# The output projection as seven products, and feed-forward products that add up in single PSUM banks

## The chip, the cores and the metric

The kernel runs on one core of a Trainium2 chip. The metric is the device time of one execution in microseconds, and lower is better. The engines are TensorE (PE, matmuls; PEld is its weight load), VectorE (DVE), ScalarE (ACT), GpSimd (POOL) and the SyncE queue (SP), which issues the loads and stores.

## The reference

One layer of a decoder block on x of 512 tokens and 1024 channels, all in float32. Two token mixers (a spatial gating unit and a gated linear attention) give m; then come the output projection, a layer norm, a feed-forward and a second layer norm:

```python
m = jax.nn.sigmoid(g_a) * y_a + jax.nn.sigmoid(g_b) * y_b
h = layer_norm(DEEPNORM_ALPHA * h + m @ w_out[l], ln1_g[l], ln1_b[l])
f = jnp.square(jax.nn.relu(h @ w_ff1[l])) @ w_ff2[l]
h = layer_norm(DEEPNORM_ALPHA * h + f, ln2_g[l], ln2_b[l])
```

m and w_out are 512 x 1024 and 1024 x 1024; w_ff1 is 1024 x 4096, w_ff2 4096 x 1024. layer_norm subtracts a row's mean, divides by the root of its variance plus 1e-5, multiplies by a gain and adds a bias for each channel.

## The kernel before, in words

Every float32 operand of a matmul is split in two parts that TensorE takes at full speed, high and low: `split` (L88) copies to the high part on ACT and subtracts on DVE for the low part. A product is then three passes: high by high, high by low, low by high (`passes`, L196). Weights come from device memory in chunks of 128 x 1024, in an order written in `_stream` (L1114); `split_to` (L127) splits a chunk into one of 7 buffers, so it runs up to 7 chunks ahead of PE, and `load_to` (L102) keeps the loads ahead of that. 

On PE, DVE, ACT and POOL the instructions stand in the order in which the code emits them (`manual_schedule`); each engine works through its own queue in that order and waits at an instruction whose inputs or buffer are not ready. The loads on SP's queue are placed by the tile framework.

The stages, with PE's work in matmuls of 128 x 128 by 512 columns:

1. Input projections and the two mixers, up to the pairs of gates (`branch`, L821, from 268 us on): for each two channel tiles e, columns of r and of g_B (24 matmuls each), after which ACT applies a SiLU or a sigmoid and DVE multiplies and adds into m (`r_take`, `gb_take`). Each tile of m is then split (L827, L855).
2. The output projection: two halves of 512 channels (`row_unit`, L199, with `out_take`, L863). For each half and each of the 4 token tiles it runs 8 x 3 matmuls into a bank of PSUM; DVE then adds alpha times x (L869) and takes row statistics (L870). After the second half `ln_apply` (L635) does the layer norm of a row: aggregate, a power on POOL (L171), and two steps of 1024 columns on DVE with gain and bias. `turn_h` (L878) transposes a token tile of h on PE (8 matmuls with the identity) into PSUM, and ACT and DVE split it into hh and hl.
3. The feed-forward's hidden layer, 512 hidden columns at a time (`block`, L922; the first in two parts of 256 tokens, L1006), and for three quarters of it (pairs 0 to 2) the second product in seven products in place of eight (`seven_products`, L967). F and w_ff2 are cut in 2 x 2 blocks; sums of blocks of w_ff2 are made on DVE by `sum_to` (L119), sums of blocks of F by `operand` (L935). A product has two token tiles of 12 matmuls. `keep` (L955) adds each product to its own accumulator in SBUF, and `together` (L993) combines the accumulators near the end. A product alternates with a hidden column job of 24 matmuls.
4. The last quarter in plain order (L1066 on) with the second layer norm. The last token tile's 1024 channels are done in pieces of 512, 384 and 128.

PSUM has 8 banks: `ps_m` 4, `ps_s` 2 and `ps_a` 2 (L84 to L86).

Of the kernel before, what the change touches and what calls it, by code (L numbers as in the profile page):

```python
# [15 lines left out]
P = 128  # L16
T = 512
# [29 lines left out]
def hybrid_block(  # L47
# [13 lines left out]
    ln1_b: bass.AP,  # L61
    ln2_g: bass.AP,
# [22 lines left out]
    ps_s = pool(ctx, "ps_s", bufs=1, space=PSUM)  # L85
    ps_a = pool(ctx, "ps_a", bufs=2, space=PSUM)  # L86
# [11 lines left out]
    raws, chunks, kept = {}, {}, {}  # L98
    lanes, ring = {0: rpool}, {lane: [] for lane in LANES}
    state = {"load": 0, "sum": 0, "split": 0}  # L100

    def load_to(n):  # L102
        while state["load"] < min(n, NCHUNK):
            i = state["load"]
            kind, lane, key, news = STREAM[i]
            if news is not None:
                ends = ring[lane]
                if len(ends) >= LANES[lane] and ends[-LANES[lane]] >= state["split"]:
                    break
                raw = lanes[lane].tile([P, 1024], F32, name=f"raw{i}", tag="raw")  # L110
                nc.sync.dma_start(raw, w_all[news])
                kept.setdefault(key, []).append(raw)
                users = [j for j in range(i + 1, NCHUNK) if STREAM[j][2] == key]
                users = [j for n_, j in enumerate(users) if all(STREAM[x][3] is None for x in users[:n_])]
                ends.append(max([i] + (users if key else [])))
            raws[i] = kept[key][-1:] if kind == "one" else kept[key][-2:]
            state["load"] = i + 1

    def sum_to(n):  # L119
        while state["sum"] < min(n, state["load"]):  # L120
            i = state["sum"]
            raw, *other = raws[i]
            if other:
                nc.vector.tensor_tensor(raw, raw, other[0], op=ALU.add if STREAM[i][0] == "sum" else ALU.subtract)  # L124
            state["sum"] = i + 1

    def split_to(n):  # L127
        n += n > ASIDE
        while state["split"] < min(n, NCHUNK):
# [8 lines left out]
            raw = raws[i][0]  # L138
# [4 lines left out]
        load_to(n + sum(LANES.values()) if 1 in lanes else n + RAW_BUFS)  # L143
# [106 lines left out]
    for i in range(4):  # L250
        raws[i] = [None]
# [542 lines left out]

    def r_take(e, t1):
# [41 lines left out]
    lnp.tile([P, 32], F32, name="pad_n")  # L837
    first_ln = ExitStack()
    ln1p = pool(first_ln, "ln1p", side="right")
    g1 = row_bcast(ln1p, ln1_g, D, "g1")  # L840
    b1 = row_bcast(ln1p, ln1_b, D, "b1")
    mstack = ExitStack()
    mpool = pool(mstack, "mpool", side="left")
    mh = mpool.tile([P, KT, T], F32R, name="mh")
    ml = mpool.tile([P, KT, T], F32R, name="ml")

    def turn(src, t, half, dh, dl):

        pt = ps_a.tile([P, 4, P], F32, name="pturn", tag="aux")
        for i in range(4):  # L850
            nc.tensor.transpose(pt[:, i, :], src[:, (half * 4 + i) * P : (half * 4 + i + 1) * P], ident)
        ks, tsl = slice(half * 4, half * 4 + 4), slice(t * P, (t + 1) * P)
        split(dh[:, ks, tsl], dl[:, ks, tsl], pt)

    for e in range(2):  # L855
        split(mh[:, e, :], ml[:, e, :], AT_[:, e, :])
    for e in range(2, KT, 2):
        branch(e)


    hh, hl = xh, xl

    def out_take(half):  # L863
        def f(t, ps):
            sl = slice(half * 512, (half + 1) * 512)
            xr = mpool.tile([P, 512], F32, name=f"xr{half}_{t}", tag="xr", bufs=3)
            nc.sync.dma_start(xr, x[t * P : (t + 1) * P, sl])
            z = bufA[:, t, sl]
            nc.vector.scalar_tensor_tensor(z, xr, ALPHA, ps, op0=ALU.mult, op1=ALU.add)  # L869
            nc.vector.bn_stats(st1[t][:, half, :], z)  # L870
            if half:
                ln_apply(
                    bufA[:, t, :], bufA[:, t, :], st1[t].rearrange("p a b -> p (a b)"), g1, b1, ln1p, f"l1{t}"
                )

        return f

    def turn_h(t):  # L878
        for half in range(2):
            turn(bufA[:, t, :], t, half, hh, hl)  # L880

    row_unit(mh, ml, out_take(0))
    at(S_O + 5, lambda: turn_h(0))
    at(S_O + 6, lambda: turn_h(1))
    row_unit(mh, ml, out_take(1))
    mstack.close()
    first_ln.close()
# [18 lines left out]
    lanes[1] = pool(seven, "rpool2", side="right", bufs=LANES[1])  # L910
    op = pool(seven, "op", side="left", bufs=2)
    sub = lambda o, x_, y_: nc.vector.tensor_tensor(o, x_, y_, op=ALU.subtract)  # L912
# [22 lines left out]
    def operand(F, p, m):  # L935
        a = lambda i, j: F[:, j - 1, :, (i - 1) * 256 : i * 256]
        x_, *y_ = {
            5: (a(1, 2), a(1, 1)),
            1: (a(1, 1), a(2, 2)),
            3: (a(1, 1),),  # L940
            4: (a(2, 2),),
            6: (a(2, 1), a(1, 1)),
            7: (a(1, 2), a(2, 2)),
            2: (a(2, 1), a(2, 2)),
        }[m]
        if y_:
            d_ = op.tile([P, 4, 256], F32, name=f"d{p}_{m}", tag="d", bufs=1)
            sub(d_, x_, y_[0])
            x_ = d_
        hi = op.tile([P, 4, 256], F32R, name=f"oh{p}_{m}", tag="oh")  # L950
        lo = op.tile([P, 4, 256], F32R, name=f"ol{p}_{m}", tag="ol")
        split(hi, lo, x_)
        return hi, lo

    def keep(p, m, t, ps):  # L955
        dst = acc[m][:, t, :]
        if p == 0 and m in (6, 7):
            h = quarter(bufA, *((1, 1) if m == 6 else (0, 0)))[:, t, :]
            nc.vector.scalar_tensor_tensor(dst, h, ALPHA, ps, op0=ALU.mult, op1=ALU.add)
        elif p == 0:  # L960
            nc.scalar.copy(dst, ps)
        else:
            nc.vector.tensor_add(dst, dst, ps)

    made = {}

    def seven_products(F, p, F_next):  # L967
# [4 lines left out]
        def job(n):  # L972
            m = ORDER[n]
# [4 lines left out]
            hi, lo = made.pop((p, n))  # L978
            u0 = take_chunks(2)
            for t in range(2):  # L980
                tsl = slice(t * P, (t + 1) * P)
                ps = ps_m.tile([P, 512], F32, name=f"m{p}_{m}_{t}", tag="ps")
                for k in range(4):
                    wh, wl = (c.rearrange("p (k n) -> p k n", k=2)[:, k % 2, :] for c in chunks[u0 + k // 2])
                    for i, (s_, m_) in enumerate(passes(hi[:, k, tsl], lo[:, k, tsl], wh, wl)):
                        nc.tensor.matmul(ps, s_, m_, start=(k == 0 and i == 0), stop=(k == 3 and i == 2))  # L986
                    if t and k % 2:
                        split_to(u0 + k // 2 + 1 + W_BUFS)
                keep(p, m, t, ps)

        return [lambda n=n: job(n) for n in range(7)]

    def together(m, t, terms, h=None):  # L993

        z = acc[m][:, t, :]
        for sign, n in terms:
            nc.vector.tensor_tensor(z, z, acc[n][:, t, :], op=ALU.add if sign > 0 else ALU.subtract)
        if h:
            nc.vector.scalar_tensor_tensor(
                z, quarter(bufA, *h)[:, t, :], ALPHA, z, op0=ALU.mult, op1=ALU.add  # L1000
            )
# [11 lines left out]
    for job in block(take_raw(F, 1)):  # L1013
        job()
# [210 lines left out]
```

## Time and profile before

| | us |
|---|---|
| median of 3 runs | 758.21 |
| lowest and highest | 758.09, 758.42 |
| the profiled execution | 757.96 |
| its span, first to last instruction | 756.2 |
| PE busy in the span | 747.2 |
| output projection on PE | 367.3 to 412.6 |
| feed-forward, hidden tokens of the second half from | 426.3 |

A row of the timeline has the start in us, the duration, the engine, the line, the operation and its tiles. The duration of a matmul is its latency; matmuls follow each other faster than that, so their cost is the step from one start to the next. A row of the list of groups has the count, the busy time, the mean of one in ns, and the idle time before it. A row of the table by windows has the stretch, then busy time (and instructions) of PE, PEld, DVE, ACT and POOL, the granted TensorE clock, the DMA share and GB/s. A row of the list of waits has who waited, for whom, us in total, times, the longest.

### The profile page before, as it was taken

Reading aid. Unit: us, or ns where it says so; the run is one execution under the profiler, and the core shown is the slowest. Engines: PE = TensorE matmul, PEld = TensorE weight load, DVE = VectorE, ACT = ScalarE, POOL = GpSimd, SP = SyncE. Lnnn points to the kernel's source line nnn. Section 1 sums busy time; section 2 is a strip of 40 time slices with the busy share of each in tenths; the row PEclk is TensorE's granted clock in tenths of the full one; section 3 lists DMA queues with packets and bytes.
Section 4 is the critical chain, followed back from the end, with each engine's and each line's share of the span. In section 5 each row is a group of like instructions: output and inputs, shape, how many; then the busy total and the mean of one; then the engine's idle time right before and its main releaser. Section 6 shows DMA issues by size and latency. Waiting matters only on the chain.

```text
span 756.2 us, 8829 instructions
## 1 busy us (share of the span) xinstructions
PE 747.2 (99%) x3498; PEld 626.8 (83%) x3498; DVE 492.8 (65%) x618; ACT 349.5 (46%) x472; POOL 29.8 (4%) x60
## 2 busy tenths in 40 slices
PE   9999999999999999999999999999999999999996
PEld 7878888888888888888888988888888888888885
DVE  8478876676575554435458544874677667777995
ACT  7475744363254735444222544454644444445300
POOL 1000000000000102000002000000000000000011
PEclk9999999999999999999999999999999999999998
DMA  8623422222142131432341423444234333534111
GB/s 341 208 73 125 137 77 80 84 84 84 36 141 75 56 126 56 144 107 84 98 158 33 171 62 107 139 140 140 86 137 141 137 112 112 164 114 166 58 56 55
DMA packets 25465, 85.15 MB, mean 113 GB/s; under 512 B 3088, under 2 KB 3344, under 8 KB 25424
## 3 DMA queue, kind: packets, MB, share of 16 engines
q1 hardware_dynamic: 25280, 84.33, 32.4%
q8 instruction: 27, 0.44, 0.2%
q10 hardware_dynamic: 144, 0.26, 0.1%
q14 instruction: 14, 0.11, 0.1%
HBM read 82.48 MB, written 2.10 MB: 112 GB/s over the span
## 4 chain that ended last, share of the span: by engine, by line
PE 96%; issue 1%; DVE 1%; DMA 0%; POOL 0%; DVEq 0%; POOLq 0%
PE f L691 22%; PE ps L213 17%; PE m L986 15%; PE f L1077 6%; PE gb L691 6%; PE r L691 6%; PE ga L691 6%; PE u L691 6%; PE qk L691 3%; PE first L272 3%; PE sc L519 2%; PE pm L744 1%; PE po L553 1%; PE po L557 1%; PE po L555 1%
## 5 line engine op out<-in xcount | busy, mean ns | idle before, releaser
L90 DVE TENSOR_TENSOR wl<-raw,wh 128x1024 fp32r<-128x1024 f32 x141 | 171.2, 1222 | 99.2 <-ACT wh L89 97.7
L89 ACT CAST wh<-raw 128x1024 fp32r<-128x1024 f32 x141 | 145.7, 1044 | 51.1 <-PE ps L213 23.7
L691 PE MATMUL f<-xh,wh 128*128 128x512 f32 (+1 forms) x288 | 105.4, 366 | 0.0
L691 PE MATMUL f<-xl,wh 128*128 128x512 f32 (+1 forms) x288 | 105.3, 365 | 0.0
L691 PE MATMUL f<-xh,wl 128*128 128x512 f32 (+1 forms) x288 | 105.2, 365 | 0.0
L986 PE MATMUL m<-wh,oh 128*128 128x512 f32 x168 | 65.4, 389 | 0.0
L986 PE MATMUL m<-wl,oh 128*128 128x512 f32 x168 | 65.4, 389 | 0.0
L986 PE MATMUL m<-wh,ol 128*128 128x512 f32 x168 | 65.4, 389 | 0.0
L691 PEld LDWEIGHTS f<-xh,wl 128*128 128x128 f32 x288 | 54.3, 189 | 8.8
L691 PEld LDWEIGHTS f<-xh,wh 128*128 128x128 f32 x288 | 54.3, 189 | 8.7
L691 PEld LDWEIGHTS f<-xl,wh 128*128 128x128 f32 x288 | 54.3, 189 | 8.6
L213 PE MATMUL ps<-wh,xh 128*128 128x512 f32 x128 | 50.4, 394 | 0.0
L213 PE MATMUL ps<-wh,xl 128*128 128x512 f32 x128 | 49.8, 389 | 0.0
L213 PE MATMUL ps<-wl,xh 128*128 128x512 f32 x128 | 49.8, 389 | 0.0
L915 ACT ACTIVATE F<-f 128x512 f32<-128x512 f32 (+1 forms) x28 | 15.0, 536 | 70.7 <-PE f L691 70.7
L124 DVE TENSOR_TENSOR raw<-raw,raw 128x1024 f32<-128x1024 f32 x30 | 36.6, 1221 | 9.1 <-DMA raw<-in_w_all 9.1
L986 PEld LDWEIGHTS m<-wh,ol 128*128 128x128 f32 x168 | 31.5, 188 | 6.6
L986 PEld LDWEIGHTS m<-wh,oh 128*128 128x128 f32 x168 | 31.5, 188 | 6.6
L986 PEld LDWEIGHTS m<-wl,oh 128*128 128x128 f32 x168 | 31.5, 188 | 6.5
L89 ACT CAST oh<-d 128x1024 fp32r<-128x1024 f32 x15 | 15.7, 1049 | 36.4 <-DVE d L912 36.4
L90 DVE TENSOR_TENSOR ol<-d,oh 128x1024 fp32r<-128x1024 f32 x15 | 18.4, 1225 | 16.7 <-ACT oh L89 16.7
L213 PEld LDWEIGHTS ps<-wh,xl 128*128 128x128 f32 x128 | 24.0, 188 | 5.1
(231 smaller groups left out, 1477.1 us busy)
## 6 DMA issues: line engine op xcount, KB each, us to landing
raw<-in_w_all SPq DMA_DIRECT2D x136, 512.0 KB, 3.3
bufB<-in_head SPq DMA_DIRECT2D x4, 512.0 KB, 7.9
xr<-in_x SPq DMA_DIRECT2D x8, 256.0 KB, 3.6
out<-bufA SPq DMA_DIRECT2D x8, 256.0 KB, 2.0
bufA<-in_head SPq DMA_DIRECT2D x3, 512.0 KB, 5.3
brow<-in_b_in SPq DMA_DIRECT2D x4, 256.0 KB, 6.4
g<-in_ln_g SPq DMA_DIRECT2D x2, 512.0 KB, 4.0
b<-in_ln_b SPq DMA_DIRECT2D x2, 512.0 KB, 4.9
```

The lines of the kernel that those rows point to most:

```text
L89: nc.scalar.copy(hi, src)
L90: nc.vector.tensor_tensor(lo, src, hi.bitcast(F32), op=ALU.subtract)
L124: nc.vector.tensor_tensor(raw, raw, other[0], op=ALU.add if STREAM[i][0] == "sum" else ALU.subtract)
L213: nc.tensor.matmul(ps, s_, m_, start=(k == 0 and i == 0), stop=(k == KT - 1 and i == 2))
L272: nc.tensor.matmul(first[e], s_, m_[:, k, :], start=(k == 0 and i == 0), stop=(k == KT - 1 and i == 2))
L519: nc.tensor.matmul(sc[:, c, 0:192], pr.kt[:, jc * P : (jc + 1) * P], pr.qt[:, jc, :], start=True, stop=True)
L553: nc.tensor.matmul(po, pr.AT[:, j, c, :], vs, start=True, stop=(c == 0))
L555: nc.tensor.matmul(po, pr.QI[:, j, c * P : (c + 1) * P], pr.S[j], start=False, stop=True)
L691: nc.tensor.matmul(ps, s_, m_, start=(k == 0 and i == 0), stop=(k == KT - 1 and i == 2))
L915: nc.scalar.activation(dst, ps, AF.Relu)
L986: nc.tensor.matmul(ps, s_, m_, start=(k == 0 and i == 0), stop=(k == 3 and i == 2))
L1077: nc.tensor.matmul(ps, s_, m_, start=(f == 0 and i == 0), stop=(f == 7 and i == 2))
```

## The change

**The projection in seven products.** m is 4 k-tiles by 2 block columns, 256 tokens by 2 block rows; w_out is stored in quarters like w_ff2. `product_of` runs one product of 2 x 12 matmuls, for the projection and the feed-forward alike. The order of products and what they add to are new:

```python
ORDER = (1, 2, 5, 6, 3, 7, 4)
PAIRED = ((0, 1), (4, 5), (2, 6), (3, 7))
...
GOES = {1: (0, 0), 2: (0, 0), 5: (1, 1), 6: (0, 1), 3: (0, 1), 7: (1, 1), 4: (1, 0)}
NEW = (1, 5, 6, 4)
```

GOES gives the quarter of the result (token half, channel half). Products 1, 6, 7 and 4 add up in the same two banks x (one for each token tile), 5 and 3 in two banks v, and 2 has banks of its own; DVE adds the state of the bank to the quarter after each product, so a bank may not be added to further before DVE has read it. `ps_s` and `ps_a` end after the gates, and the four banks x and v take their place; v also takes the transposed tiles.

```diff
+    def accumulators(m, name):
+        if m in (1, 6, 7, 4):
+            if m == 1:
+                sums["x"] = [ps_t.tile([P, 512], F32, name=f"mx{name}_{t}", tag=f"x{t}") for t in range(2)]
+            return sums["x"], m == 1
+        if m in (5, 3):
+            if m == 5:
+                sums["v"] = [ps_t.tile([P, 512], F32, name=f"mv{name}_{t}", tag=f"v{t}") for t in range(2)]
+            return sums["v"], m == 5
+        return [ps_m.tile([P, 512], F32, name=f"m{name}_{t}", tag="ps") for t in range(2)], True
```

**Operands.** The gates are done in the order PAIRED, so that both channel tiles of a k-tile are there; after each pair the operands of that k-tile are made: three blocks are split as they are, and four sums of 256 columns are made and split (`summed`). The blocks of w_out and w_ff2 are subtracted in place in four held buffers (`A0`, `A1`, `B0`, `B1`), and the chunk stream has 14 chunks for the projection where there were 8.

```diff
+    def summed(k):
+        a = lambda i, j: AT_[:, k + 4 * (j - 1), (i - 1) * 256 : i * 256]
+        d = [temp(f"ms{k}_{i}").rearrange("p (m t) -> p m t", m=2) for i in range(2)]
+        (s1, s2), (s4, s3) = [(x_[:, 0, :], x_[:, 1, :]) for x_ in d]
+        nc.vector.tensor_tensor(s1, a(2, 1), a(2, 2), op=ALU.add)
+        for o, x_, y_ in ((s2, s1, a(1, 1)), (s4, a(1, 2), s2), (s3, a(1, 1), a(2, 1))):
+            nc.vector.tensor_tensor(o, x_, y_, op=ALU.subtract)
+        for i in range(2):
+            split(mh[:, 2 * i : 2 * i + 2, k, :], ml[:, 2 * i : 2 * i + 2, k, :], d[i])
```

**The first layer norm.** Token tiles 0 and 1 are normalised on ACT without gain and bias; these are applied on channels after the transpose, by eight ACT instructions of 128 x 128 in PSUM for a tile, and much later in rows on DVE for the residual. Tiles 2 and 3 keep the form in rows.

```diff
+    def turn_h(t):
+        for half in range(2):
+            pt = ps_t.tile([P, 4, P], F32, name="pturn", tag=f"v{half}")
+            for i in range(4):
+                e = half * 4 + i
+                nc.tensor.transpose(pt[:, i, :], bufA[:, t, e * P : (e + 1) * P], ident)
+            for i in range(4 if t < 2 else 0):
+                e = half * 4 + i
+                g_, b_ = ln1c[:, e : e + 1], ln1c[:, 8 + e : 9 + e]
+                nc.scalar.activation(pt[:, i, :], pt[:, i, :], AF.Identity, bias=b_, scale=g_)
+            ks, tsl = slice(half * 4, half * 4 + 4), slice(t * P, (t + 1) * P)
+            split(hh[:, ks, tsl], hl[:, ks, tsl], pt)
+
+    def project_take(m, t, ps):
+        i, j = GOES[m]
+        dst, tt = quarter(bufA, i, j)[:, t, :], 2 * i + t
+        if m in NEW:
+            xr = mpool.tile([P, 512], F32, name=f"xr{m}_{t}", tag="xr", bufs=3)
+            nc.sync.dma_start(xr, x[tt * P : (tt + 1) * P, j * 512 : j * 512 + 512])
+            nc.vector.scalar_tensor_tensor(dst, xr, ALPHA, ps, op0=ALU.mult, op1=ALU.add)
+        else:
+            nc.vector.tensor_add(dst, dst, ps)
+        if m in (2, 3, 7, 4):
+            stats(tt, j)
+        if m == 3:
+            rest_of_stats(tt)
+            if t:
+                normalise(0)
+        if m == 7:
+            if t:
+                normalise(1)
+            else:
+                turn_h(0)
+        if m == 4:
+            st = st1[tt].rearrange("p a b -> p (a b)")
+            ln_apply(bufA[:, tt, :], bufA[:, tt, :], st, *rows1["gb"], lnp, f"l1{tt}")
+            if t == 0:
+                turn_h(1)
```

**The feed-forward.** Its 3 x 7 products keep their number and size, with the new order, operands and banks; `keep` adds every product to its quarter at once, and `together` and its accumulators go. The gain and bias of tiles 0 and 1 are multiplied and added in rows on DVE during the second hidden block.

```diff
-        pieces = ((0, 512), (512, 512)) if t < NT - 1 else ((0, 512), (512, 384), (896, 128))
+        pieces = ((0, 512), (512, 512)) if t < NT - 1 else ((0, 512), (512, 256), (768, 256))
```

Besides, the weights of the low-rank gate (`als`) take one of the 7 weight buffers early on and are split in whole, and the scratch area for DMA is smaller.

**Where instructions moved.** On DVE, from the last gate's addition into m (first row). Before, wl is the low part of a chunk, ml that of m; L869 and L870 are the addition and the statistics of a token tile:

```order
L817 TENSOR_TENSOR bufA<-bufA,gb_2829 128x512
L90 TENSOR_TENSOR wl_2834<-raw_2727,wh_2833 128x1024
L90 TENSOR_TENSOR ml<-bufA,mh 128x512
L869 SCALAR_TENSOR_TENSOR bufA<-xr_0_2866,ps_0_2841 128x512
L870 BN_STATS st_0_2360<-bufA 128x6
L869 SCALAR_TENSOR_TENSOR bufA<-xr_1_2895,ps_1_2870 128x512
L870 BN_STATS st_1_2361<-bufA 128x6
```

And after the change, from the same addition to the first of product 1 (L959); L130 subtracts chunks of weights, L910 and L912 make the sums of m:

```order
L867 TENSOR_TENSOR bufA<-bufA,gb_2848 128x512
L130 TENSOR_TENSOR raw_2441<-raw_2691,raw_2441 128x1024
L91 TENSOR_TENSOR wl_2853<-raw_2439,wh_2852 128x1024
L91 TENSOR_TENSOR ml<-bufA,mh 128x256
L910 TENSOR_TENSOR ms_0_2861<-bufA 128x256
L912 TENSOR_TENSOR ms_0_2861<-ms_0_2861,bufA 128x256
L912 TENSOR_TENSOR ms_1_2862<-bufA,ms_0_2861 128x256
L912 TENSOR_TENSOR ms_1_2862<-bufA 128x256
L91 TENSOR_TENSOR ml<-ms_0_2861,mh 128x2x256
L91 TENSOR_TENSOR ml<-ms_1_2862,mh 128x2x256
L91 TENSOR_TENSOR ml<-bufA,mh 128x256
L959 SCALAR_TENSOR_TENSOR bufA<-xr_0_2892,mxo_0_2878 128x512
```

Ten instructions stand between the last gate and the projection's first addition where there were two.

On DVE at the end of the projection, before: the third token tile's second half with its layer norm, the low parts of a turned tile (xl), then chunks of weights:

```order
L869 SCALAR_TENSOR_TENSOR bufA<-xr_2_3092,ps_2_3067 128x512
L870 BN_STATS st_2_2362<-bufA 128x6
L638 BN_AGGR mv_l_3096<-st_2_2362 128x2
L168 TENSOR_SCALAR rs_l_3097<-mv_l_3096 128x1
L640 SCALAR_TENSOR_TENSOR bufA<-bufA,mv_l_3096,g_2372 128x1024
L646 SCALAR_TENSOR_TENSOR bufA<-bufA,rs_l_3097,b_2374 128x1024
L90 TENSOR_TENSOR xl<-pturn,xh 128x4x128 x2
L90 TENSOR_TENSOR wl_3125<-raw_2951,wh_3124 128x1024
```

After, from product 7's second tile (mxo is a bank x) over product 4's first tile with its layer norm to the low parts of token tile 1:

```order
L961 TENSOR_TENSOR bufA<-bufA,mxo_1_2879 128x512
L930 BN_STATS st_3_2343<-bufA 128x6
L959 SCALAR_TENSOR_TENSOR bufA<-xr_0_3182,mxo_0_2878 128x512
L930 BN_STATS st_2_2342<-bufA 128x6
L640 BN_AGGR mv_l_3186<-st_2_2342 128x2
L175 TENSOR_SCALAR rs_l_3187<-mv_l_3186 128x1
L642 SCALAR_TENSOR_TENSOR bufA<-bufA,mv_l_3186,mf_2962 128x1024
L648 SCALAR_TENSOR_TENSOR bufA<-bufA,rs_l_3187,mf_2964 128x1024
L91 TENSOR_TENSOR xl<-pturn,xh 128x4x128 x2
```

Here xl is token tile 1, and the hidden layer's first part needs it; half a product of PE's work (12 matmuls) stands between its turn and that part where a whole group (24 matmuls) stood.

On PE, the first turn before and after (pturn is the transposed tile):

```order
L213 MATMUL ps_1_3017<-wh_2935,mh 128x512
L213 MATMUL ps_1_3017<-wl_2936,mh 128x512
L213 MATMUL ps_1_3017<-wh_2935,ml 128x512
L851 MATMUL pturn<-ident,bufA 128x128 x8
L213 MATMUL ps_2_3067<-wh_2761,mh 128x512
```

```order
L832 MATMUL mxo_0_2878<-wh_2989,mh 128x512
L832 MATMUL mxo_0_2878<-wl_2990,mh 128x512
L832 MATMUL mxo_0_2878<-wh_2989,ml 128x512
L945 MATMUL pturn<-ident,bufA 128x128 x8
L832 MATMUL mxo_1_2879<-wh_2953,mh 128x512
```

The turn of token tile 0 now stands behind product 7's first tile, that of tile 1 behind product 4's first tile.

More of the change, by code (lines that the diff above doesn't have):

```diff
@@ L96, in hybrid_block @@
     ASIDE = NCHUNK - 3
-    raws, chunks, kept = {}, {}, {}
-    lanes, ring = {0: rpool}, {lane: [] for lane in LANES}
+    chunks, kept, ring = {}, {}, []
+    held, held_to = {}, {}
     state = {"load": 0, "sum": 0, "split": 0}
@@ L104, in load_to @@
             i = state["load"]
[L105 to L108, printed above, removed]
+            c, own, *_ = STREAM[i]
+            if c is not None and own is None:
+                if len(ring) >= RAW_BUFS and ring[-RAW_BUFS] >= state["split"]:
                     break
[L110 to L116, printed above, removed]
+                kept[i] = rpool.tile([P, 1024], F32, name=f"raw{i}", tag="raw")
+                ring.append(i)
+            elif c is not None:
+                if "pool" not in held or held_to.get(own, -1) >= state["split"]:
+                    break
+                kept[i] = held[own] = held["pool"].tile([P, 1024], F32, name=f"raw{i}", tag=own)
+                held_to[own] = max(j for j in range(i, min(i + 40, NCHUNK)) if STREAM[j][3] == STREAM[i][3] and own in STREAM[j][2:])
+            if c is not None:
+                nc.sync.dma_start(kept[i], w_all[c])
             state["load"] = i + 1
@@ L121, in sum_to @@
             i = state["sum"]
-            raw, *other = raws[i]
-            if other:
-                nc.vector.tensor_tensor(raw, raw, other[0], op=ALU.add if STREAM[i][0] == "sum" else ALU.subtract)
+            _, own, dst, _, less = STREAM[i]
+            if dst is not None:
+                raw = held[dst]
+                if less:
+                    x_, y_ = (held[a] if a else kept[i] for a in less)
+                    nc.vector.tensor_tensor(raw, x_, y_, op=ALU.subtract)
+                kept[i] = raw
             state["sum"] = i + 1
@@ L142, in split_to @@
             state["split"] = i + 1
[L143 removed]
+        load_to(n + RAW_BUFS + 2)
     xh = xpool.tile([P, KT, T], F32R, name="xh")
@@ L843, in hybrid_block @@
     mpool = pool(mstack, "mpool", side="left")
[L844 to L858, printed above, removed]
-    hh, hl = xh, xl
[L863 to L876, printed above, removed]
+    mh = mpool.tile([P, 6, 4, 256], F32R, name="mh")
@@ L977, in job @@
                 made[p + 1, 0] = operand(F_next, p + 1, ORDER[0])
[L978 to L989, printed above, removed]
-        return [lambda n=n: job(n) for n in range(7)]
[L993 to L1001, printed above, removed]
+            product_of(f"{p}_{ORDER[n]}", ORDER[n], made.pop((p, n)), keep(p))
+        return [lambda n=n: job(n) for n in range(7)]
     F = fp.tile([P, 2, 4, T], F32, name="F0", tag="F")
@@ L1118, in _stream @@
     n = 15 * 4
-    out = [("one", 0, None, None)] * 4 + [("one", 0, None, c) for c in range(n)]
+    out = [(None, None, None, None, None)] * 4 + [(c, None, None, None, None) for c in range(n - 8)]
     f1 = n
@@ L1142, in _stream @@
             out += take(1 + (i == 0)) + product
-    out += [("one", 0, None, f2 + 8 * PAIRS + c) for c in range(8 * (DF // 1024 - PAIRS))]
+    out += [(f2 + 8 * PAIRS + c, None, None, None, None) for c in range(8 * (DF // 1024 - PAIRS))]
     return out
```

219 lines of the change are left out of this document (118 added, 101 removed).

## The prediction

> **What bounds the kernel now.** I read the page first: PE's row, then the list of what PE waits for.
>
> ```profile
> PE 747.2 (99%) x3498; PEld 626.8 (83%) x3498; DVE 492.8 (65%) x618; ACT 349.5 (46%) x472; POOL 29.8 (4%) x60
> ```
>
> ```profile
> PE wu L248 <- POOL bal L294: 1.1, 1, 1.1
> PE pt L408 <- PE ps L213: 0.6, 1, 0.6
> ```
>
> Nothing here is long: PE is busy 99% of the span and never waits in the stages that the change touches. So the time is PE's own work, as long as the other engines stay ahead. The chain prices that work.
>
> ```profile
> 367.46 32.64 PE ps L213 x144
> ...
> 470.64 5.44 PE m L986 x24
> ```
>
> 144 matmuls in 32.64 us and 24 in 5.44 us are both 0.2267 us for a matmul of 512 columns. The table by windows shows how far DVE is from PE: in the last gates, in the output projection, in the feed-forward.
>
> ```profile
> 290.00:367.40 77.40, 77.40 (x355) 64.16 (x354) 34.85 (x42) 35.94 (x51) 3.55 (x8) 1.00 0.29 100
> 367.40:411.00 43.60, 43.60 (x202) 36.28 (x201) 27.08 (x36) 10.54 (x13) 4.56 (x3) 1.00 0.29 96
> ```
>
> ```profile
> 465.00:704.50 239.50, 239.50 (x1058) 198.30 (x1057) 172.55 (x166) 122.34 (x153) 0.00 (x0) 1.00 0.39 132
> ```
>
> DVE (third number) has 27.08 us of work in the projection's 43.60 and 172.55 of 239.50 in the feed-forward.
>
> **What PE saves.** The projection goes from 8 x 24 = 192 matmuls to 7 x 24 = 168. That is 24 x 0.2267 = 5.44 us less. The feed-forward keeps its 21 products. At the end the last row's pieces change.
>
> ```profile
> 742.52 0.33 PE L1077 MATMUL f<-wh,Fs 128*128 128x384 f32 x1
> ...
> 746.71 0.22 PE L1077 MATMUL f<-wh,Fs 128*128 128x128 f32 x1
> ...
> 749.22 0.28 PE L1077 MATMUL f<-wh,xl 128*128 128x128 f32 x1
> ```
>
> ```profile
> 423.33 0.36 PE L691 MATMUL f<-xh,wh 128*128 128x256 f32 x1
> 423.53 0.28 PE L691 MATMUL f<-xl,wh 128*128 128x256 f32 x1
> 423.65 0.29 PE L691 MATMUL f<-xh,wl 128*128 128x256 f32 x1
> ```
>
> The pieces of 384 and 128 columns take 742.52 to 749.33, 6.8 us. Two of 256 take 48 x 0.12 = 5.8 us (0.12 is the step from 423.53 to 423.65). The last piece's add and statistics on DVE double in width, about 0.14 us each by the next two rows. Net -0.8 us.
>
> ```profile
> L1078 DVE TENSOR_TENSOR bufB<-bufB,f 128x128 f32<-128x128 f32 x1 | 0.3, 289 | 1.5 <-PE f L1077 1.5
> ```
>
> ```profile
> L480 DVE TENSOR_TENSOR dr<-dr,k 128x256 f32<-128x256 f32 x4 | 1.7, 425 | 0.1
> ```
>
> **What DVE pays.** Before, the projection's 192 matmuls used 8 chunks of weights; now 168 use 14, of which 8 are first made by a subtraction. DVE works strictly in the order of its queue. Its prices by the step from one start to the next:
>
> ```profile
> 478.96 1.22 DVE L124 TENSOR_TENSOR raw<-raw,raw 128x1024 f32<-128x1024 f32 x1
> 480.10 1.22 DVE L90 TENSOR_TENSOR wl<-raw,wh 128x1024 fp32r<-128x1024 f32 x1
> ...
> 486.07 0.68 DVE L959 SCALAR_TENSOR_TENSOR bufB<-bufA,m 128x512 f32<-128x512 f32 x1
> 486.72 1.22 DVE L90 TENSOR_TENSOR wl<-raw,wh 128x1024 fp32r<-128x1024 f32 x1
> ```
>
> 1.14 us for 1024 columns, 0.65 for 512, some 0.37 for 256. Let 0 be the first matmul of product 1:
>
> ```profile
> 367.30 0.39 PE L213 MATMUL ps<-wh,mh 128*128 128x512 f32 x1
> ```
>
> Nothing on PE ahead of it changes, and DVE is up to date there: the operands cost it 4 x (7 x 0.37 + 2 x 0.65) = 16 us in place of 8 x 0.65 = 5, and the window from 290 has 42 us free. But the last gate ends at 0 too, and its work cannot start earlier: PE's result at 0.2, the sigmoid 0.7 (row below), DVE at 0.9. From there to the addition of product 3's first tile its queue holds 34 instructions: 14 of 1024 columns (10 splits, 4 sums: 16.0 us), 12 of 512 (7.9), 2 statistics (1.4), 6 of 256 (2.2). That is 27.5 us and 0.3 of dependent gaps: DVE is there at 28.8. PE has finished that tile at 24.6. **DVE is 4.2 us late**, and the rest follows from that. The single bank for products 5 and 3 bites first: product 3's second tile may not be added to it before DVE has read product 5's, at 25.2; PE is there at 24.5 and waits 0.8.
>
> Then row 0's layer norm, priced from today's:
>
> ```profile
> 394.70 0.69 DVE L869 SCALAR_TENSOR_TENSOR bufA<-xr,ps 128x512 f32<-128x512 f32 x1 [1.36 <-PE ps L213]
> 395.42 0.69 DVE L870 BATCH_NORM_STATS2 st<-bufA 128x6 f32<-128x512 f32 x1
> 396.15 0.21 DVE L638 BATCH_NORM_AGGREGATE mv_l<-st 128x2 f32<-128x12 f32 x1
> 396.39 0.15 DVE L168 TENSOR_SCALAR rs_l<-mv_l 128x1 f32<-128x1 f32 x1
> 396.46 1.28 DVE L640 SCALAR_TENSOR_TENSOR bufA<-bufA,mv_l,g 128x1024 f32<-128x1024 f32 x1
> ```
>
> ```profile
> 396.63 1.52 POOL L171 TENSOR_TENSOR rs_l<-rs_l,nhalf 128x1 f32<-128x1 f32 x1 [95.34 <-DVE rs_l L168]
> ```
>
> ```profile
> L171 POOL TENSOR_TENSOR rs_sg<-rs_sg,nhalf 128x1 f32<-128x1 f32 x4 | 2.2, 551 | 63.9 <-DVE rs_sg L168 63.9
> ...
> L654 POOL TENSOR_SCALAR rs_sg<-mv_sg,rs_sg 128x1 f32<-128x1 f32 x4 | 1.1, 264 | 0.4
> ```
>
> ```profile
> L673 ACT ACTIVATE bufB<-bufB,rs_sg 128x1024 f32<-128x1024 f32 x4 | 4.9, 1233 | 0.0
> ...
> L815 ACT ACTIVATE gb<-gb,cols_sb 128x512 f32<-128x512 f32 x8 | 5.5, 689 | 22.1 <-PE gb L691 22.1
> ```
>
> 28.8 + 1.84 on DVE (394.70 to 396.54) + 1.52 on POOL = 32.2. The same power takes 0.551 where DVE is idle, and 1.52 where a long DVE instruction runs: it ended 0.41 after that instruction. Now two splits run there back to back, so I let POOL's second instruction (0.264 alone) end after the second, at 33.2; alone it would be 32.5. Then 1.23 on ACT, and PE may turn row 0 at **34.6** (or 33.8). Without waits PE would be there after 11 half products, at 29.9.
>
> [...]
>
> From that turn to the first hidden tile, DVE and ACT alternate:
>
> ```profile
> 415.48 1.04 PE L851 MATMUL pturn<-ident,bufA 128*128 128x128 f32 x8
> ```
>
> ```profile
> L580 ACT ACTIVATE bufB<-po,ss 128x256 f32<-128x256 f32 x16 | 6.8, 470 | 0.2 <-POOL ss L171 0.2
> ```
>
> ```profile
> L915 ACT ACTIVATE F<-f 128x256 f32<-128x256 f32 x8 | 3.1, 383 | 9.6 <-PE f L691 9.6
> ```
>
> ```profile
> L89 ACT CAST xh<-pturn 128x512 fp32r<-128x512 f32 x8 | 4.4, 584 | 13.8 <-PE pturn L851 13.8
> ```
>
> The scale and shift on channels is 8 new ACT instructions for each of two rows, 128x128 in PSUM; no row shows one. Half of a 256-column step is 0.10 (584 less 383, halved), so 0.28 without and 0.37 with a pointer (470). I take 0.37, and 0.03 between, as each waits for the last. A row then costs ACT 2 x (4 x 0.40 + 0.55) = 4.3. Row 0: 34.6 + 0.7 + 4.3 = 39.6; two casts and splits of weights behind it, DVE free at 43.0. Only then come, in DVE's order: the addition and statistics of product 7's second tile, the same of product 4's first (2.8), aggregate and scalar (0.4), the 1024-column step (1.28), the wait for POOL (0.4), the next (1.28), and at last row 1's low part, 0.65: **49.7**. Meanwhile PE does two half products, a turn, a half product (10.2 us, and a wait of 1.7 for row 1's normalisation on ACT) and stands at 46.5, as the hidden tile's second matmul needs that low part: 3.2 us of wait. Four hidden parts and two turns later (4 x 2.88 + 2 x 1.04 = 13.6) the second half of the hidden tokens starts at 63.3. Before it is 423.33 + 24 x 0.12 = 426.3, or 59.0. **The stage is 4.3 us longer:** 5.4 saved, 9.7 of waits. With POOL's lower price and 0.28 the same count gives 61.9 (+2.9); with DVE 3% slower, 64.5 (+5.5).
>
> **What costs nothing.** From there the feed-forward hides the rest: sums fall from 10 to 8 a pair, operands from 5 subtractions to 4, the last additions (20 x 0.68) go, ten copies of ACT's become DVE's additions (6.5 us) and four 1024-column steps come for the late scale and shift (4.6 us); DVE had 67 us free. Its banks are used once more after a full hidden job, 8.2 us of slack. If that cover went, DVE's lag beyond 8.2 us would fall on PE. The loads behind the held buffers on SP's queue wait for DVE's splits at 18.0 and 22.4, and what stands behind them is wanted at 25.4 or later. The early low-rank weights only change their place.
>
> **The sum.** Against the profiled execution, 757.96 (span 756.2): +4.3 - 0.8 = +3.5, between +2.1 and +4.7. The median is 758.21, 0.25 above; on it the forecast is 761.7.
>
> **Rivals.** First, the gain arrives: PE gets 5.4 and 0.8 us, **752.0**. It decides at the low part of row 1: DVE would have to be through it by about 40, not 49.7. For it: PE waits nowhere today, DVE has 16.5 us free in this stage, and the loads are early. Against it: the count above, in which no step is dearer than today's, and the strict order of the queue. 0.16.
>
> Second, DVE goes through its queue about 8% faster than its steps today; the same count then starts the second half near 59: **757 to 759.5**, no change. Against it: the steps are the same to 1% wherever I looked. 0.15.
>
> Third, PE's waits halve its clock. After the last matmul the granted clock fell:
>
> ```profile
> 751.00:752.00 1.00, 0.00 (x0) 0.00 (x0) 1.00 (x3) 0.00 (x0) 0.68 (x1) 0.91 0.00 0
> 752.00:753.00 1.00, 0.00 (x0) 0.00 (x0) 1.00 (x2) 0.00 (x0) 0.00 (x0) 0.50 0.00 0
> ```
>
> 0.91 over one microsecond is a fall at 751.8, 2.3 us after PE's end at 749.5. Waits of 3.9 and 3.2 us are longer. At half speed the first would be swallowed by PE's later waits; behind the second a hidden part takes 2.88 us more: **764.6**. 0.15. [...]
>
> **How the numbers follow.** Forecast 0.54, rivals 0.16, 0.15, 0.15. A measurement tells about 0.2%, 1.5 us, from no change. Faster 0.16, within 0.15, slower 0.54 + 0.15 = 0.69. The range leaves out the first rival and little else: 757.0 to 765.0; the forecast's own is 760.3 to 762.9.
>
> **What would show it.** Right: PE waits in product 3, 3 to 4 us before the first turn, 1 to 2 before the second, about 3 at the first hidden part, and no waits later; POOL's power near 1.5; the scale and shift near 0.37. Wrong: the first turn follows its half product without a gap, or DVE reaches product 3's addition before 25, or PE waits in the feed-forward.

## The result and the profile after

| | before | after |
|---|---|---|
| median, us | 758.13 (6 runs) | 762.05 (6 runs) |
| lowest and highest | 757.87, 758.42 | 761.51, 763.62 |
| the profiled execution, its span | 757.96, 756.2 | 761.6, 759.5 |

The ratio is 1.0055, with a 95% interval of 1.0045 to 1.0065: 0.55% slower. The runs of the changed kernel lie 2.1 us apart, those of the kernel before 0.55.

The page, first the busy times. PE is busy 4.2 us less than the 747.2 of before (24 matmuls fewer, but some at a clock of 0.50, see below), in a span that is 3.3 us longer.

```profile
PE 743.0 (98%) x3474; PEld 622.3 (82%) x3474; DVE 502.7 (66%) x640; ACT 362.5 (48%) x485; POOL 29.7 (4%) x62
```

The list of what PE waits for has three rows that were not there before (in all, times, the longest), all in the stretch that the change made new.

```profile
PE pturn L945 <- ACT bufA L937: 5.2, 2, 3.2
PE f L693 <- DVE xl L91: 1.3, 1, 1.3
...
PE mvo L832 <- DVE bufA L959: 0.2, 1, 0.2
```

The table by windows for the gates, the projection with the first hidden tiles, and the feed-forward (PE, PEld, DVE, ACT, POOL, then the granted clock). Only the middle stretch has a PE below its length, and only there is the clock below 1.00.

```profile
290.00:366.00 76.00, 76.00 (x349) 63.02 (x348) 43.15 (x64) 38.91 (x60) 3.55 (x8) 1.00 0.26 87
366.00:429.00 63.00, 56.25 (x293) 47.37 (x292) 55.20 (x75) 33.29 (x53) 6.08 (x6) 0.97 0.53 190
465.00:707.00 242.00, 242.00 (x1069) 200.44 (x1068) 169.64 (x167) 117.59 (x143) 0.00 (x0) 1.00 0.36 122
```

The chain that ended last has the same piece in both kernels, behind the last turn: the rest of the hidden tiles, 264 matmuls. Its start is called the link below. Before:

```profile
423.57 47.06 PE f L691 x264
```

After, with the start of the low part of row 1 that the first hidden tile waits for:

```profile
415.99 0.69 DVE xl L91
416.73 3.01 PE f L693 x23
...
427.65 47.06 PE f L693 x264
```

Product 1 starts at 367.30 before and at 367.49 after (each kernel's zero in what follows):

```profile
367.49 0.39 PE L832 MATMUL mxo<-wh,mf 128*128 128x512 f32 x1
```

So the link comes 56.3 after zero before and 60.2 after: the stage is 3.9 us longer. From the link to the end of the span it is 756.2 - 423.57 = 332.6 before and 759.5 - 427.65 = 331.9 after, 0.8 less. With the 0.2 us of a later zero that is the 3.3 us of the spans.

Where the stage's time goes, on the timelines of DVE, POOL, ACT and PE:

```profile
391.62 0.68 DVE L959 SCALAR_TENSOR_TENSOR bufA<-xr,mvo 128x512 f32<-128x512 f32 x1
392.21 0.68 DVE L959 SCALAR_TENSOR_TENSOR bufA<-xr,mxo 128x512 f32<-128x512 f32 x1
...
395.08 0.68 DVE L959 SCALAR_TENSOR_TENSOR bufA<-xr,mxo 128x512 f32<-128x512 f32 x1
395.68 0.68 DVE L961 TENSOR_TENSOR bufA<-bufA,mvo 128x512 f32<-128x512 f32 x1
396.39 0.69 DVE L930 BATCH_NORM_STATS2 st<-bufA 128x6 f32<-128x512 f32 x1
...
397.45 2.36 DVE L91 TENSOR_TENSOR wl<-raw,wh 128x1024 fp32r<-128x1024 f32 x2
...
401.48 0.68 DVE L961 TENSOR_TENSOR bufA<-bufA,mxo 128x512 f32<-128x512 f32 x1
402.19 0.69 DVE L930 BATCH_NORM_STATS2 st<-bufA 128x6 f32<-128x512 f32 x1
```

```profile
397.60 1.48 POOL L178 TENSOR_TENSOR rs_l<-rs_l,nhalf 128x1 f32<-128x1 f32 x1 [96.13 <-DVE rs_l L175]
399.18 0.76 POOL L656 TENSOR_SCALAR rs_l<-mv_l,rs_l 128x1 f32<-128x1 f32 x1
401.65 0.55 POOL L178 TENSOR_TENSOR rs_l<-rs_l,nhalf 128x1 f32<-128x1 f32 x1 [1.71 <-DVE rs_l L175]
402.30 0.27 POOL L656 TENSOR_SCALAR rs_l<-mv_l,rs_l 128x1 f32<-128x1 f32 x1
```

```profile
399.97 1.24 ACT L937 ACTIVATE bufA<-bufA,rs_l 128x1024 f32<-128x1024 f32 x1 [2.86 <-POOL rs_l L656]
401.96 1.82 ACT L949 ACTIVATE pturn<-pturn,ln1c 128x128 f32<-128x128 f32 x4 [0.75 <-PE pturn L945]
...
406.64 1.99 ACT L90 CAST wh<-raw 128x1024 fp32r<-128x1024 f32 x2
```

```profile
401.27 1.09 PE L945 MATMUL pturn<-ident,bufA 128*128 128x128 f32 x8 [3.16 <-ACT bufA L937]
...
409.83 1.71 PE L945 MATMUL pturn<-ident,bufA 128*128 128x128 f32 x8 [1.99 <-ACT bufA L937]
...
416.73 0.39 PE L693 MATMUL f<-xl,wh 128*128 128x256 f32 x1 [1.33 <-DVE xl L91]
```

DVE reaches product 3's first addition 28.2 after zero. From there statistics, POOL's two instructions and ACT's normalisation stand in a line up to the first turn at 33.8, while two splits of weights go on beside them on DVE. POOL's power and its small instruction take 1.48 and 0.76 us for row 0, beside these splits, and 0.55 and 0.27 for row 1, beside the addition at 401.48 and the statistics at 402.19.

By microseconds, the clock falls to half right behind the second wait:

```profile
410.00:411.00 1.00, 1.00 (x7) 1.00 (x7) 0.97 (x3) 0.27 (x1) 0.00 (x0) 0.57 0.86 279
411.00:412.00 1.00, 1.00 (x5) 0.91 (x4) 0.99 (x2) 0.93 (x3) 0.00 (x0) 0.50 0.83 266
412.00:413.00 1.00, 1.00 (x3) 0.76 (x3) 0.90 (x2) 0.94 (x3) 0.00 (x0) 0.50 0.69 209
413.00:414.00 1.00, 1.00 (x5) 0.77 (x4) 1.00 (x2) 0.93 (x4) 0.76 (x1) 0.72 0.71 279
```

0.43 + 0.50 + 0.50 + 0.28 = 1.7 us of PE's work lost. The sum of the stage: at the first turn, the second turn, the first hidden part and product 3 the steps from start to start are 3.3, 2.2, 1.5 and 0.4 us longer than without the waits (each step is some 0.16 us longer than its wait: a matmul's duration of 0.39 less its step of 0.23), in all 7.4; with the half clock 9.1; less the 5.4 us saved 3.7, of 3.9 measured.

### The profile page after: what moved, and what is told of

It reads as the page before. It is cut to its first block, busy times and chain, and to the rows that moved or that the text cites. A ratio compares the mean times of both kernels' runs of the same rounds, so it can differ in the third digit from the quotient of the medians.

```text
span 759.5 us, 8842 instructions
## 1 busy us (share of the span) xinstructions
PE 743.0 (98%) x3474; PEld 622.3 (82%) x3474; DVE 502.7 (66%) x640; ACT 362.5 (48%) x485; POOL 29.7 (4%) x62
## 4 chain that ended last, share of the span: by engine, by line
PE 92%; DVE 4%; issue 1%; ACT 1%; DMA 1%; POOL 0%; DVEq 0%; ACTq 0%
PE f L693 23%; PE ps L220 11%; PE mx L832 9%; PE f L1127 6%; PE gb L693 6%; PE r L693 6%; PE ga L693 6%; PE u L693 6%; PE mv L832 4%; PE qk L693 3%; PE first L277 3%; PE m L832 2%; PE sc L521 2%; DVE wl L91 1%; PE pm L746 1%
## 5 line engine op out<-in xcount | busy, mean ns | idle before, releaser
L91 DVE TENSOR_TENSOR wl<-raw,wh 128x1024 fp32r<-128x1024 f32 x147 | 178.1, 1222 | 107.3 <-ACT wh L90 105.8
L90 ACT CAST wh<-raw 128x1024 fp32r<-128x1024 f32 x147 | 151.5, 1044 | 37.9 <-PE mx L832 9.9
L130 DVE TENSOR_TENSOR raw<-raw,raw 128x1024 f32<-128x1024 f32 x32 | 39.0, 1218 | 2.8 <-DMA raw<-in_w_all 2.8
L832 PE MATMUL mx<-wh,oh 128*128 128x512 f32 x96 | 37.3, 389 | 0.0
L832 PE MATMUL mx<-wl,oh 128*128 128x512 f32 x96 | 37.3, 389 | 0.0
L832 PE MATMUL mx<-wh,ol 128*128 128x512 f32 x96 | 37.3, 389 | 0.0
L220 PEld LDWEIGHTS ps<-wl,xh 128*128 128x128 f32 x128 | 24.0, 188 | 4.9
L220 PEld LDWEIGHTS ps<-wh,xh 128*128 128x128 f32 x128 | 24.0, 188 | 4.8
L90 ACT CAST oh<-d 128x1024 fp32r<-128x1024 f32 x12 | 12.6, 1049 | 29.1 <-DVE d L1028 29.1
L693 PE MATMUL u<-xh,wh 128*128 128x512 f32 x64 | 25.9, 405 | 0.0
L693 PE MATMUL ga<-xh,wh 128*128 128x512 f32 x64 | 25.9, 404 | 0.0
```

Source lines behind the costliest of these rows:

```text
L90: nc.scalar.copy(hi, src)
L91: nc.vector.tensor_tensor(lo, src, hi.bitcast(F32), op=ALU.subtract)
L130: nc.vector.tensor_tensor(raw, x_, y_, op=ALU.subtract)
L832: nc.tensor.matmul(ps, s_, m_, start=(begins and k == 0 and i == 0), stop=(k == 3 and i == 2), skip_group_check=True,)
```

## The experiments

The queue theory is the prediction's: DVE's queue in order sets when each row of h is ready. The scale theory: the new channel instructions on ACT, and what waits for them, are the cost. The clock theory: the half clock behind the waits is the loss. All medians below stand beside a median of the kernel before of 757.99 to 758.17 on the same chip.

**The clock kept up, two places** (`e1_warm`). Ahead of `turn_h(0)` 12, ahead of `turn_h(1)` 8:

```diff
+    def keep_busy(n, name):
+        kb = ps_m.tile([P, 512], F32, name=name, tag="ps")
+        for i in range(n):
+            nc.tensor.matmul(kb, ones_r, mh[:, 0, 0:2, :]..., start=(i == 0), stop=(i == n - 1))
```

> The changed kernel with 12 extra matmuls of 512 columns ahead of the first turn and 8 ahead of the second (into a free bank, result unused), so that TensorE is busy in most of its two waits. Queue theory: the first turn, the second turn and row 1's low part on DVE come when they came, so the fastest runs stay near 761.5; the granted clock stays 1.00, the 1.8 us that the half clock took after the second turn become wait at the first hidden part (1.3 to some 3), and what the slower runs had above the fastest (up to 2.1 us) is gone: median 761.3 to 761.8. Clock theory: the half clock makes the loss, so without it the time falls to about 759.8.

Measured: 762.53 (762.42 to 763.77), ratio 1.0061 [1.0047, 1.0075]. The two waits for the turns are 0.4 in all, the wait at the hidden part is 2.9:

```profile
PE f L693 <- DVE xl L91: 2.9, 1, 2.9
PE pturn L950 <- ACT bufA L937: 0.4, 1, 0.4
```

And the fall has not gone; it moved behind that wait, where nothing swallows it:

```profile
416.00:417.00 1.00, 0.52 (x4) 0.52 (x5) 1.00 (x3) 0.95 (x1) 0.00 (x0) 1.00 0.00 0
417.00:418.00 1.00, 1.00 (x8) 1.00 (x8) 1.00 (x2) 0.00 (x0) 0.00 (x0) 0.72 0.00 0
418.00:419.00 1.00, 1.00 (x7) 1.00 (x6) 1.00 (x2) 0.00 (x0) 0.00 (x0) 0.50 0.00 0
```

The hidden part starts when it did (49.2 after zero both times, when the low part is there); the expected time missed by the fall behind it. As the clock still fell once, this run does not settle the clock theory; a third place does.

**The clock kept up, three places** (`e5_warm3`):

```diff
                 turn_h(1)
+            else:
+                keep_busy(9, "kb2")
```

> The first warm kernel with 9 more extra matmuls of 512 columns (2.0 us) behind the projection's last one, where its clock had fallen behind the wait of 2.9 us at the first hidden part. Queue theory: DVE ends row 1's low part when it did, the hidden part starts some 49 us after zero, and as no clock falls now nothing is added behind it: 761.3 (760.7 to 761.7), all runs within 0.6. Clock theory, as first stated (the loss is the half clock's): 759.8 or less. If a fall costs nothing wherever it is: 762.5, as with two places.

Measured: 761.5 (761.27 to 762.0), clock 0.997 to 0.999 in all runs. With no fall by that clock (the change's runs have 0.990 to 0.996) the changed kernel takes what its fastest runs took. So the clock is not the loss. Its fall is the likely reason why the runs of the changed kernel spread upward, by up to 2 us: they show granted clocks from 0.996 down to 0.990, the lowest in the longest run. The profiled run is one of the shorter, so no trace shows it.

**Weights split later** (`e2_ahead`), from product 5 on 4 chunks ahead of PE:

```diff
-                    split_to(u0 + k // 2 + 1 + W_BUFS)
+                    split_to(u0 + k // 2 + 1 + (4 if name in ("o5", "o6", "o3", "o7", "o4") else W_BUFS))
```

> The changed kernel with the weights split 4 chunks ahead of TensorE in place of 7 from product 5 to product 4 (the same splits, later). DVE has 4 instructions of 1024 columns (4 x 1.14 = 4.6 us) fewer ahead of product 3's first addition and one more behind it. Queue theory: that addition comes when TensorE has the tile, about 24.6 after zero in place of 28.2, the first turn some 3.3 us sooner, the hidden part as much: about 758.5 (757.5 to 759.5). Scale theory (the 16 channel instructions on ACT and what waits for them are the cost): the first turn is sooner but ACT's 4.8 us a row stand in the chain, the hidden part moves by less than 1 us: 760.8 to 761.6. Clock theory: with the first wait gone the clock does not fall: 759.8, wherever DVE is.

Measured: 758.25 (757.85 to 760.15), ratio 1.0007 [0.9998, 1.0016]: 3.8 us less than the change, by order alone; the link is 56.7 after zero (423.88 less 367.22), where it was 60.2. DVE now waits for PE at product 3, and the first turn's wait is 0.2 of the 2.2:

```profile
391.90 0.69 DVE L961 TENSOR_TENSOR bufA<-bufA,mvo 128x512 f32<-128x512 f32 x1 [0.36 <-PE mvo L832]
```

```profile
PE pturn L945 <- ACT bufA L937: 2.2, 2, 2.0
PE f L693 <- DVE xl L91: 1.3, 1, 1.3
```

The clock fell here too, for 3.4 us behind the wait of 2.0, and ACT has the same channel instructions. The queue theory stands, the two others fall as the main cause.

**No scale and shift on channels** (`e3_noscale`):

```diff
-            for i in range(4 if t < 2 else 0):
+            for i in range(0):
```

> The changed kernel without the 16 scale and shift instructions on channels: gain and bias of token tiles 0 and 1 are left out on the way to the hidden layer. The first turn and all before it stay. Queue theory: DVE, which stood idle 1.55 and 1.65 us for ACT's two casts of row 0, goes on 3.2 us sooner to row 2's additions and row 1's low part: 758.3 (757.8 to 759.5), so the two mechanisms are in one chain and the waits ahead of the first turn stay at 3.2. Scale theory: the cost of ACT's 16 x 0.46 = 7.3 us goes, 754.5 to 757.

Measured: 760.26 (760.12 to 762.78), ratio 1.0036 [1.0024, 1.0049]: 1.8 us less than the change; 758.3 was expected. ACT's next casts of weights waited for buffers that product 7 held, and product 7 ran at half clock here (from 400.9, behind the first wait); DVE waited for the casts:

```profile
404.97 1.05 ACT L90 CAST wh<-raw 128x1024 fp32r<-128x1024 f32 x1 [1.67 <-PE mxo L832]
```

```profile
406.05 1.23 DVE L91 TENSOR_TENSOR wl<-raw,wh 128x1024 fp32r<-128x1024 f32 x1 [2.02 <-ACT wh L90]
```

So I overlooked that PE hands buffers back. The waits ahead of the first turn stay at 3.1, as the queue theory has it.

**Gain and bias of rows 0 and 1 in rows** (`e9_rows`), that part of the change undone:

```diff
         if m == 3:
-            rest_of_stats(tt)
-            if t:
-                normalise(0)
+            ln_apply(bufA[:, tt, :], bufA[:, tt, :], st1[tt]..., *rows1["gb"], lnp, f"l1{tt}")
```

> The changed kernel with gain and bias of token tiles 0 and 1 in rows on DVE, as tiles 2 and 3 have them, so the 16 channel instructions, ACT's two normalisations and the late steps on rows are gone. Queue theory: row 0's turn comes 0.8 us sooner, but DVE has 4 x 1.2 us more and two more waits of 0.44 for POOL against 3.2 us less of waiting for ACT: row 1's low part and the hidden part 2.7 us later, 764 (763 to 765.5). Scale theory: without the channel instructions 754.5 to 758.

Measured: 767.69 (767.64 to 767.77), ratio 1.0127 [1.0111, 1.0142]. The first turn is 33.0 after zero (33.8 in the changed kernel), the first hidden part 2.1 us later, the link 3.2 later, with a half clock (0.50 from 418.87 to 422.28) that nothing swallows. The span is 6.5 us longer than the change's, and 3.6 of that comes behind the link, where nothing was meant to change. The chain shows each product of the feed-forward at 5.59 us, without any wait:

```profile
709.47 5.59 PE mx L832 x24
```

A small tile of four buffers was gone, and the operands' buffers lay 128 bytes lower.

**The same with 128 bytes of padding** (`e10_rows_pad`), `pad_n` with 144 columns for 112.

> The kernel with rows 0 and 1 in rows, with 128 bytes more padding ahead of the operand buffers. In the run without it each product of the feed-forward took 5.59 us in place of 5.44 with no wait anywhere; its buffers had moved down by 128 bytes, off a multiple of 256, as a small tile was gone. If the place of the buffers is the cause: the products take 5.44 again, 22 x 0.15 = 3.3 us less, 764.3, and what is left above the changed kernel is the stage's 2.9 us. If the cause is something else that the rows brought: 767.7 again.

Measured: 764.31 (764.17 to 764.74), ratio 1.0083 [1.0069, 1.0097].

```profile
706.56 5.44 PE mx L832 x24
```

The place was the cause of the slower products, and the rows cost 764.3 where the channels cost 762.05. Against rows on DVE the channels are the cheaper form, the opposite of what the scale theory says, though they do stand in the chain: without any scale 1.8 us went.

**The changed kernel with 128 bytes less** (`e11_pad80`), `pad_n` with 80 columns for 112 and nothing else.

> The changed kernel with 128 bytes less padding ahead of the operand buffers, nothing else. If the place of the buffers sets the pace of the products: 5.59 us a product in the feed-forward, 761.6 + 3.3 = 764.9 (764 to 766.5). If not: as the changed kernel, 761.5 to 763.6.

Measured: 766.48 (766.25 to 767.53), ratio 1.0114 [1.01, 1.0127].

```profile
708.99 5.59 PE mx L832 x24
```

Its profiled execution is the longest of its runs, with a span of 765.5, 6.0 above the change's: 3.6 of that behind the link, of which 21 products of 0.15 us are 3.2 and the hidden jobs between them, at 5.46 for 5.44, the rest; and 2.3 in the stage (link 62.4 after zero, not 60.2), where the clock fell twice, the second time for 6.82 us around the first hidden part (from 416.04 to 422.86). The expectation counted 22 products where 21 stand behind the link, but the size of that part is the expected one; I had not allowed for another fall.

**The tail's pieces alone, on the kernel before** (`e4_tail`):

```diff
-        pieces = ... ((0, 512), (512, 384), (896, 128))
+        pieces = ... ((0, 512), (512, 256), (768, 256))
```

> The kernel before with only the last row's pieces changed, 512, 256 and 256 in place of 512, 384 and 128. All theories: 0.8 us less than before, 757.3 (0.5 to 1.0 less).

Measured: 757.21 (756.93 to 757.42), ratio 0.9987 [0.9978, 0.9996]: 1.0 us less.

**A new order for rows 0 and 1** (`e6_weave`), on top of the later splits. `normalise(1)` follows `turn_h(0)`; for product 7 the splits come behind the addition, one chunk in place of two; and:

```diff
+                turn_h(1, lambda: nc.vector.scalar_tensor_tensor(row, row, mv[:, 0:1], g, op0=ALU.subtract, op1=ALU.mult))
+                nc.vector.scalar_tensor_tensor(row, row, rs, b, op0=ALU.mult, op1=ALU.add)
```

> The kernel with weights split 4 chunks ahead, and three more changes of order: row 1 is normalised on ACT ahead of product 7's splits, product 7's second tile is added ahead of its splits (one chunk now, not two), and row 1's low parts come ahead of row 2's two steps of 1024 columns on DVE, the first of which stands between them. Queue theory: the second turn loses its wait of 2.0, row 1's first low part is made some 41 us after zero in place of 45.5, the wait at the hidden part falls from 1.3 (and 1.7 of half clock) to about 1: stage 3.5 us shorter, 754.5 (753.5 to 756). Scale theory: ACT's 9.4 us for two rows bound the chain, no more than 1.5 us are won: 756.7 or more. Clock theory: without a wait of 2 us there is no fall, 1.7 us less: 756.5.

Measured: 759.04 (758.19 to 759.54), ratio 1.0011 [1.0002, 1.002]. A miss. The part that was changed did as expected: the hidden tile's second matmul is 41.5 after zero (49.2 in the change) with a wait of 0.6. But a new wait stands at the fourth turn:

```profile
PE pturn L947 <- DVE xl L91: 3.2, 1, 3.2
...
PE f L693 <- DVE xl L91: 0.6, 1, 0.6
```

```profile
420.32 0.38 ACT L1009 ACTIVATE F<-f 128x256 f32<-128x256 f32 x1 [7.25 <-issue]
```

ACT stands 7 us at the first hidden tile's square, with row 2's casts behind it. Its buffer F (bytes 151040 to 167424 of a partition in this kernel) lies over row 3's gain and bias (from 160256 on), and these are read to the end of row 3's layer norm (DVE, 418.95 to 420.23). The profile names no releaser; ACT goes on 0.09 us behind that end.

**The same for rows 2 and 3** (`e8_weave2`): row 2's casts ahead of the squares, and row 3's steps behind row 2's low parts. Product 4's second tile is also added ahead of all but one split, so the run does not part the two.

```diff
+    def in_between(e, tsl, ps):
+        first[e] = ps
+        if e in (0, 2):
+            turn_h(2 + e // 2)
+        if e == 0:
+            last_row()
+            split_to(u0 + 4)
```

> The kernel before this, and the same again for rows 2 and 3: product 4's second tile is added ahead of all but one split, row 2's casts and low parts come ahead of row 3's two steps of 1024 columns and of the first hidden tiles' squares, whose buffer lies where row 3's gain and bias lay. Queue theory: the wait of 3.2 at the fourth turn falls to some 0.6, no wait of 2 us is left and no fall of the clock; the second half of the hidden tokens starts some 55.2 after zero (59.0 in the kernel before): 754.3 (753.3 to 755.8). If the fourth turn's wait is not from this order: 757 to 758.5.

Measured: 755.1 (754.51 to 755.22), ratio 0.9959 [0.9946, 0.9971]: 3.0 us faster than the kernel before and 7 faster than the change, with the same matmuls.

```profile
PE pturn L947 <- DVE bufA L1000: 0.9, 1, 0.9
...
PE f L693 <- DVE xl L91: 0.6, 1, 0.6
...
PE pturn L947 <- ACT bufA L939: 0.2, 1, 0.2
```

```profile
421.30 47.06 PE f L693 x264
```

The link is 53.5 after zero (367.85), 2.8 sooner than before; the expectation had 3.8. The wait at the fourth turn is 0.9, for the 0.6 expected. The clock was 0.997 to 0.999.

## Why the prediction was right

The time, 762.05 for 761.7, and the way there. By its steps:

1. PE's saving of 5.4 us came, and the tail's 0.8: 0.8 in the two traces for the link to the end, feed-forward included, and 1.0 with the tail alone. So the feed-forward in single banks cost nothing, as forecast: PE has 242.00 of 242.00 in the window from 465.
2. "DVE is there at 28.8": 28.2. Its steps of 1024 columns were the forecast's 1.14 (nine splits and five sums, for ten and four, at one price). Most additions of 512 took 0.60 (391.62 to 392.21 and 395.08 to 395.68) for 0.65; the 12 instructions of 512 and the gaps behind them took 7.7 for 8.2 and the two statistics 1.2 for 1.4, which is the difference. The bank of products 5 and 3 took 0.2 (0.4 from start to start) in place of 0.8, as DVE was sooner. Later splits moved this addition and took the loss away (758.25), so the queue is shown as the cause.
3. The first turn at 34.6, or 33.8 with POOL's small instruction alone: 33.8, but not by that way; that the time fell on the other bound is luck. The power took 1.48, for 1.52. The small one took 0.76 and ended at 399.94, 0.13 behind the second split (397.45 + 2.36 = 399.81): it ended after that split, as I had let it. Of the 0.8 us, 0.6 are DVE's earlier arrival (point 2); 0.2 are smaller gaps, as it took 4.3 us from the addition to POOL's end, for 4.4, and 1.3 from there to the turn, for 1.4. The wait was 3.2, for 3.9.
4. The second turn's wait of 1.7: 2.0. The scale and shift take 0.46 us from start to start (1.82 for four, 0.43 each), for 0.40; a row costs ACT 4.7, from 401.96 to 406.64, for 4.3. The term was 0.4 too small.
5. Row 1's low part at 49.7 and a wait of 3.2 at the hidden part: the tile goes on at 49.2, after a wait of 1.3. The other 1.7 us passed at half clock just ahead of it: PE came that much later to a result that was not there yet. The forecast had both as alternatives, and they were one time.
6. The stage at +4.3: +3.9.

The first rival, the gain arrives, failed where the prediction said that it is decided, at row 1's low part; with DVE through it at about 41 and rows 2 and 3 in order, 3.0 of its 6.2 us do arrive (755.1). The second, a DVE 8% faster, came only for the shortest steps (point 2), 0.6 us in all. The third was right in its mechanism and wrong in its price. The clock did fall, to 0.50 from 410.14 to 413.56; in the profiled execution that cost nothing, as it lay ahead of a longer wait, and in other runs probably up to 2 us, by the spread of the runs and the narrower one with three kept places (761.27 to 762.0). The prediction read a fall 2.3 us after PE's end and took the longer waits for enough; the wait of 3.16 us ahead of the first turn brought none (below).

What stays open: some 0.2 us of the stage, and the 0.5 us by which product 1 of the last kernel above starts later than the kernel before's (367.85 for 367.30), ahead of everything that was changed.

## What to carry to other kernels

Work taken off PE is worth what the next engine's queue lets through: count what stands in that queue ahead of the one result that PE needs, not how much of the engine is free. Here the same instructions in another order were worth 7 us, after the saving of 5.4 had come out as a loss of 3.9. Work with a late due time, such as weights split ahead, belongs behind a chain that PE waits for; and when one wait goes, look for the next one in the same chain before calling the job done.

## What was not expected of the hardware

**The half clock lasted 3.4 us or twice that.** In half-microsecond windows the half clock of the changed kernel lasts from 410.14 (0.64 granted in the first) to 413.56: 3.42 us. With rows on DVE the falls are at 401.80 and 418.87, and the rises between and behind them at 408.63 and 422.28:

```profile
401.50:402.00 0.50, 0.00 (x0) 0.00 (x0) 0.50 (x1) 0.04 (x1) 0.00 (x0) 0.80 0.11 41
408.50:409.00 0.50, 0.50 (x4) 0.41 (x3) 0.50 (x2) 0.00 (x0) 0.00 (x0) 0.87 0.00 0
418.50:419.00 0.50, 0.42 (x3) 0.42 (x4) 0.50 (x2) 0.00 (x0) 0.00 (x0) 0.87 0.00 0
422.00:422.50 0.50, 0.50 (x5) 0.50 (x5) 0.47 (x1) 0.00 (x0) 0.00 (x0) 0.72 0.97 385
```

So the clock was at half for 6.83 and 3.41 us, with 10.24 between the two: 2, 1 and 3 times 3.41. With 128 bytes less the stretches at half clock are 402.38 to 405.80 and 416.04 to 422.86, 3.42 and 6.82, again with 10.24 between. I read this as a grid of 3.41 us within each run; no run shows what makes it. Laid on that grid, the 3.41 us ahead of the fall at 410.14 held 1.99 us of idle time, and with later splits, ahead of the fall at 406.97, 1.97; the wait of 3.16 ahead of the first turn lay across a boundary, 1.79 and 1.37, and no fall came. Where the first 3.41 us at half clock held idle time themselves, another 3.41 at half clock followed: 1.33 us of idle time with rows on DVE (from 401.80), 0.83 with 128 bytes less (from 416.04). Where they held none, full clock (1.00) followed, as at 413.56. So behind the wait of 1.99 us PE lost 1.7 us of work to the clock, and behind the longer one of 3.16 nothing; by that reading the difference is where the grid lay in the run.

**The place of the buffers changed the pace of matmuls by 2.8%.** With the feed-forward operands 128 bytes off a multiple of 256 (from byte 119168 of a partition, in place of 119296 = 466 x 256), 24 matmuls took 5.59 us in place of 5.44, without a wait, and one product after another. Two pairs of kernels that differ in padding alone show it: rows with and without it, and the change with 128 bytes less. Which access is slower is open, and so is any place but these two.

**Two small POOL instructions beside long DVE ones** took 1.48 and 0.76 us, beside short ones 0.55 and 0.27. Each ended just behind the DVE instruction that ran when it started: the power at 399.08, 0.41 behind the first split (397.45 + 1.22), the small one 0.13 behind the second; with later splits it was 0.40 and 0.13. The splits read two tiles in SBUF (raw and wh), while row 1's pair, at 0.55 and 0.27, ran beside an addition with one of its inputs in PSUM (mxo, 401.48) and statistics with one input. In the kernel before, the power took 0.98 us beside an instruction of 0.74 that reads two tiles in SBUF (POOL at 721.42, DVE L1089 at 721.26) and ended 0.40 behind it, so length alone does not decide. That two inputs in SBUF decide is my reading of these rows; no run was made for it.
